# The first products of a hybrid encoder layer: backward gate first, forward gate in pieces of 256 and 272 columns, meta tokens normed ahead of the rows

## The chip, the core and the metric

The kernel runs on one core of a Trainium2 chip. The metric is the device time of one execution in microseconds (us), the median of several runs; shorter is better. Before the change the median of three runs is 1535.19 us (1533.58 to 1536.26). A profile is one further execution, recorded by the hardware.

Five engines work side by side, each through its own instructions in order: PE (TensorE, matrix products; its weight loads are listed apart as PEld), DVE (VectorE), ACT (ScalarE), POOL (GpSimd) and SP (SyncE, which here only starts transfers). PE writes to PSUM, eight banks of 128 partitions x 512 fp32 numbers; everything else lies in SBUF.

## What is computed

One layer: 16 learned meta tokens ahead of 1024 rows of width 1024, an RMSNorm, one wide input projection, neighbourhood attention beside a bidirectional gated recurrence (HGRN2), and an MLP. The change touches the first microseconds alone: the norm, and the two gate projections of the recurrence's first head.

```python
h = jnp.concatenate([meta_tokens, x], axis=1)          # 16 + 1024 rows
a = rms_norm(h, norm_mix)                              # h * rsqrt(mean(h*h) + eps) * g
(q_na, k_na, v_na, q_hg, z_f, z_b, i_hg, g_hg, gate_na, gate_hg) = split_cols(a @ w_in)

def gates(z, lb):                                      # z_f: 16 + 1024 rows, z_b: the 1024 rows
    log_f = logaddexp(log(lb), log1p(-lb) + log_sigmoid(z))
    return -expm1(log_f), log_f                        # k, and the log of the forget factor f
```

In the kernel f is `oml * sigmoid(z) + lb` and k is `oml * sigmoid(-z)`. The backward direction needs no meta rows, the forward direction does.

## The kernel before

The 1024 rows are kept as two halves of 512 tokens, normed and transposed: `aT[0]` and `aT[1]`, each a pair (high part in fp32r, and the rest, "low") of tiles 128 x 8 x 512; the first half has 64 more columns, of which 16 hold the meta tokens, behind the 512. A product of 128 output columns with n tokens is a sum over k = 0..7, and each k takes three matmuls into one PSUM bank: high weights x high tokens, high x low, low x high (`mm3`, L120 to L124). A block of 128 columns of `w_in` (512 KB) is loaded as `raw`; ACT copies it to `hi`, DVE or POOL makes `lo` of the difference.

`start` (L512) does what must come first. Rows arrive as eight tiles `xt[0..7]` of 128 rows, started by SP (L526), with the two gate blocks (forward `C_ZF`, then backward `C_ZB`) between the fourth and the fifth; the meta tokens are `xt[8]`, called `xm`, started by ACT (L528). For a tile, `square` sums its squares (ACT, L544, or DVE, L546), `root` takes the power -1/2 on POOL (L555), `scale` multiplies on DVE (L551), `turn` transposes on PE (L565), `evict` writes the high part from PSUM on ACT (L575) and the low part on DVE (L576). PE fills the time before the first rows are there with transposes of the identity into a bank nobody reads (`keep_warm`, L561): 36, and 6 ahead of each further tile.

Then, in the order in which the code is written (inside `manual_schedule` that order holds on every engine):

1. forward gate, first half: 8 k of 512 columns, with the transposes of chunks 6 and 7 of the first half between them (a chunk is one k of the four tiles of a half);
2. backward gate, first half: 6 k;
3. chunk by chunk the second half is transposed and evicted (chunk 0 to 7), with the last 2 k of the backward gate and the first 5 k of the forward gate's second half between the chunks; after the first chunk ACT evicts the first gate (two sigmoids, L220 and L221, from PSUM; DVE does the rest, L222 and L225), and after the fourth it squares the meta tokens;
4. the meta tokens are transposed (L656) and written to `aT[0]` (L657 to L659);
5. `rest` (L663): the remaining k of the forward gate's second half; the forward gate of the 16 meta tokens alone, 24 matmuls of 16 columns; the backward gate's second half, 8 k.

Behind that the first head's query projection (`C_Q`) and the rest of the kernel follow. Chunks of the second half go through the four banks of tag "a", so the transposes of chunk 4 wait until chunk 0's bank has been evicted by ACT and DVE, chunk 6 for chunk 2's, and so on. Two banks each have the tags "mm" and "mx".

Of the kernel before, what the change touches and what calls it, by code (L numbers as in the profile page):

```python
# [9 lines left out]
F32 = mybir.dt.float32  # L10
# [38 lines left out]
def layer(ctx: ExitStack, tc: tile.TileContext, x, meta, w_in, w_na, w_hg, w_o, w_up, w_dn,  # L49
# [23 lines left out]
    def bank(tag, name):  # L73
        return banks[tag].tile([P, 4, P], F32, tag=tag, name=name)
# [25 lines left out]
    def load_raw(src, kc):  # L100
        raw = wp.tile([P, KC, P], F32, tag="raw", name="raw")
        sp.dma_start(raw[:, :kc], src.rearrange("(k p) c -> p k c", p=P))
        return raw
# [17 lines left out]
    def mm3(ps, lh, ll, rh, rl, first, last):  # L121
        pe.matmul(ps, lh, rh, start=first, stop=False)  # L122
        pe.matmul(ps, lh, rl, start=False, stop=False)  # L123
        pe.matmul(ps, ll, rh, start=False, stop=last)  # L124
# [79 lines left out]
    def gates_of(hd, hp, tiles, done=()):  # L204
# [30 lines left out]
        if hd == 0:  # L235
            yield
            for n_ in range(5):
                d, ps, t0, n, nm = done[n_]
                ev, mev = gate(d)
                if nm:  # L240
                    mev(ps[:, n:])
                if n:
                    ev(ps[:, :n], t0, n)
                yield
            return
        zf = proj_steps(C_ZF + hd * P, *gate(0))
# [251 lines left out]

    firsts, blocks = [], {}

    def first_products(d, h, tag, n=TH):

        nm = NM if n == NM else 0
        c0 = TH if nm else 0
        ps = bank(tag, "mm").rearrange("p a b -> p (a b)")[:, :n]
        firsts.append((d, ps, h * TH, n - nm, nm))
        hi, lo = blocks[d]
        for k in range(KC):
            mm3(ps, hi[:, k], lo[:, k], *(q[:, k, c0:c0 + n] for q in aT[h]), k == 0, k == KC - 1)
            yield  # L510

    def start(gates):  # L512
# [12 lines left out]
        def load_x(i):  # L525
            sp.dma_start(xt[i][:, :D], x[i * P:(i + 1) * P, :])  # L526
# [2 lines left out]
        act.dma_start(g_col, g_mix)  # L529
        act.dma_start(lt.rearrange("p a b c -> p (a b c)"), lbl)  # L530
        act.dma_start(gain_sb, gain)
        for i in range(4):
            load_x(i)
        raws = [load_raw(w_in[:, c:c + P], KC) for c in (C_ZF, C_ZB)]
        for i in range(4, 8):
            load_x(i)

        def square(i, eng=act):
            t = xt[i]
# [38 lines left out]
        def some(steps, n):  # L578
            for _ in range(n):
                next(steps)  # L580

        def block(d):
            blocks[d] = [wp.tile([P, KC, P], F32R, tag=t, name=t) for t in ("hi", "lo")]
            act.copy(blocks[d][0], raws[d])

        def low(d, eng, c):
            hi, lo = blocks[d]
            eng.tensor_tensor(lo[:, c], raws[d][:, c], hi[:, c].bitcast(F32), op=ALU.subtract)
# [1 line left out]
        A, B = slice(0, 4), slice(4, 8)  # L590
        lts = lt.rearrange("p a b c -> p (a b c)")
        mh, ml = (t[:, :, TH:TH + NM] for t in aT[0])
        for k in range(6):
            pts[0, k] = bank("a" if k < 4 else "mx", "pt")
        for i in range(4):
            keep_warm(6 if i else 36)
            square(i)
            root(i)
            scale(i)
            turn(i, range(6))  # L600
        block(0)
        low(0, dve, A)
        f0 = first_products(0, 0, "mm")
        evict(0, 0)
        evict(0, 1)
        for k in range(6):
            some(f0, 1)
            if k < 2:
                chunk(0, k + 6)
            if k == 0:  # L610
                low(0, dve, B)
            evict(0, k + 2)
            if k == 0:
                block(1)
                low(1, pool, A)
                low(1, pool, B)
            if k == 3:
                dve.tensor_tensor(mx, lt[:, :, 0], lt[:, :, 1], op=ALU.max)
                for q in range(2):
                    pool.tensor_tensor(lt[:, :, q], lt[:, :, q], mx, op=ALU.subtract)  # L620
        some(f0, 2)
        square(4)
        root(4)
        act.activation(lts, lts, AF.Exp)
# [10 lines left out]
            scale(i)  # L635
        pool.tensor_tensor(lb_sb, lt[:, :, 0], mx, op=ALU.mult)
        pool.tensor_tensor(oml_sb, lt[:, :, 1], mx, op=ALU.mult)
        b0 = first_products(1, 0, "mx")
        some(b0, 6)
        f1 = first_products(0, 1, "mx")  # L640
        for k in range(KC):
            chunk(1, k)
            evict(1, k)
            if k == 0:
                next(gates)
            if k == 3:
                square(8)
                root(8)
                scale(8)
            if k < 2:  # L650
                some(b0, 1)
            if k > 2:
                some(f1, 1)
        ptm = bank("mm", "ptm")[:, 0].rearrange("p (k t) -> p k t", t=NM)
        for k in range(KC):
            pe.transpose(ptm[:, k], xt[8][:, k * P:(k + 1) * P], ident[:NM, :NM])  # L656
        dve.tensor_tensor(am, ptm, fap(g_col, 0, [[1, KC], [0, NM]]), op=ALU.mult)  # L657
        act.copy(mh, am)
        dve.tensor_tensor(ml, am, mh.bitcast(F32), op=ALU.subtract)  # L659
        p0s.close()  # L660
        return f1

    def rest(gates, f1):  # L663

        list(f1)
        next(gates)
        next(gates)
        list(first_products(0, 0, "mm", NM))
        next(gates)
        early[C_Q] = block_of(C_Q)  # L670
        list(first_products(1, 1, "mm"))
        next(gates)

    early = {}
# [971 lines left out]
```

## Time and profile before

| what | us |
|---|---|
| median of 3 runs | 1535.19 |
| the profiled execution, from outside | 1532.35 |
| its span in the trace | 1530.6 |
| PE busy | 1507.1 |
| DVE busy | 1029.2 |
| ACT busy | 657.9 |
| POOL busy | 379.6 |

The profiled execution took 1.75 us more than its span (1532.35 less 1530.6); times inside the trace count from the span's start. It was 2.84 us shorter than the median of the three timed runs, so a saving is worked out against its own time and then set against that median.

In rows of the timeline the columns are start in us, duration in us, engine, line, operation, output<-inputs, shape, count and, in brackets, the idle time just before with what ended it. The duration of a matmul has its pipeline in it: what one costs is read from start to start. Rows of one tile, or of one line, give the durations of a group as min/median/max in ns. A DMA row ends with the us from issue to landing. "SPq", "ACTq" are the issues of a transfer on SP and ACT.

### The profile page before, as it was taken

The page shows a single profiled execution, that of the slowest core. Times are in us where ns is not written, and L with a number is a line of the kernel's source. Part 1 is how long each engine was busy: PE and PEld are TensorE (multiplying, and loading weights), DVE is VectorE, ACT ScalarE, POOL GpSimd, SP SyncE. Part 2 cuts the span into 40 slices and gives each one's busy share as a digit, 9 for nine tenths or more (in the row PEclk, how much of TensorE's full clock was granted, in tenths as well). Part 3 has the DMA queues.
Part 4 walks back from the last instruction along what each step waited for, and adds up shares of the span by engine and source line. Part 5 has one row for each costly group of instructions (what it writes and reads, how often), then busy time and mean ns, then how long its engine had stood idle before and what let it go on. Part 6 is the DMA issues. An engine that isn't in the chain of part 4 may idle for free.

```text
span 1530.6 us, 23534 instructions
## 1 busy us (share of the span) xinstructions
PE 1507.1 (98%) x9242; PEld 1258.1 (82%) x9242; DVE 1029.2 (67%) x1602; ACT 657.9 (43%) x1168; POOL 379.6 (25%) x355
## 2 busy tenths in 40 slices
PE   9999999999999999999999999999999999999998
PEld 8888888878888887888888887888888888888886
DVE  6776666654876877666476358877777544877876
ACT  6231313125665676334133135455555533434444
POOL 3313131315414400011000122433344200231142
PEclk9999999999999999999999999999999999999999
DMA  4211111113123227445756123544444577573324
GB/s 167 59 29 43 42 44 32 54 35 124 61 69 113 80 69 251 137 131 164 256 163 222 46 92 117 175 153 153 152 154 154 209 261 235 192 233 111 96 83 151
DMA packets 142591, 195.61 MB, mean 128 GB/s; under 512 B 8192, under 2 KB 90240, under 8 KB 142480
## 3 DMA queue, kind: packets, MB, share of 16 engines
q1 hardware_dynamic: 133216, 172.53, 34.4%
q10 hardware_dynamic: 7088, 14.24, 2.4%
q0 software_dynamic: 2176, 7.34, 1.3%
q8 instruction: 72, 1.18, 0.3%
q14 instruction: 39, 0.32, 0.1%
HBM read 139.56 MB, written 54.53 MB: 127 GB/s over the span
## 4 chain that ended last, share of the span: by engine, by line
PE 90%; DVE 5%; issue 2%; ACT 2%; DMA 1%; POOL 1%; ACTq 0%; POOLq 0%; DVEq 0%
PE mm L122 11%; PE mm L123 11%; PE mm L124 11%; PE mm L1368 5%; PE pa L1368 4%; PE pb L875 4%; PE pb L876 4%; PE pb L877 4%; PE pb L1368 4%; PE pc L1368 4%; PE pc L876 3%; PE pc L875 3%; PE pc L877 3%; PE pa L877 2%; PE pa L876 2%
## 5 line engine op out<-in xcount | busy, mean ns | idle before, releaser
L122 PE MATMUL mm<-aT,hi 128*128 128x512 f32 (+2 forms) x640 | 230.2, 360 | 2.3 <-DVE QX L746 1.5
L124 PE MATMUL mm<-aT,lo 128*128 128x512 f32 (+2 forms) x640 | 226.8, 354 | 0.0
L123 PE MATMUL mm<-aT,hi 128*128 128x512 f32 (+2 forms) x640 | 226.0, 353 | 0.6 <-DVE aT L576 0.6
L122 PEld LDWEIGHTS mm<-aT,hi 128*128 128x128 f32 x640 | 120.7, 189 | 16.9 <-issue 1.7
L123 PEld LDWEIGHTS mm<-aT,hi 128*128 128x128 f32 x640 | 120.9, 189 | 13.7 <-DVE aT L576 1.2
L124 PEld LDWEIGHTS mm<-aT,lo 128*128 128x128 f32 x640 | 120.8, 189 | 13.4
L97 DVE TENSOR_TENSOR dl<-ur,dh 128x1024 fp32r<-128x1024 f32 x54 | 71.0, 1316 | 87.3 <-ACT dh L96 87.1
L96 ACT CAST dh<-ur 128x1024 fp32r<-128x1024 f32 x54 | 56.9, 1054 | 166.5 <-issue 91.1
L112 ACT CAST hi<-raw 128x1024 fp32r<-128x1024 f32 x34 | 35.7, 1051 | 96.7 <-PE mm L123 68.4
L1173 DVE TENSOR_TENSOR wl<-raw,wh 128x512 fp32r<-128x512 f32 x50 | 41.0, 824 | 36.4 <-ACT wh L1172 36.3
L1177 ACT ACTIVATE uv<-uv 128x512 f32<-128x512 f32 x48 | 30.4, 632 | 80.0 <-DVE uv L1285 48.9
L1173 DVE TENSOR_TENSOR wl<-sx,wh 128x512 fp32r<-128x512 f32 x70 | 61.1, 883 | 3.4 <-ACT wh L1172 3.3
L1172 ACT CAST wh<-sx 128x512 fp32r<-128x512 f32 x70 | 42.2, 619 | 42.4 <-PE pc L876 23.9
L1458 POOL TENSOR_TENSOR w<-w,tt 128x512 f32<-128x512 f32 x16 | 23.4, 1461 | 132.9 <-DVE tt L1457 113.2
L301 POOL TENSOR_TENSOR Y<-X,TN 128x512 f32<-128x512 f32 x20 | 34.2, 1711 | 84.6 <-DVE X L298 84.6
L801 DVE CUSTOM_DVE_ANT_0 pr<-nsc,NB 128x432 f32<-128x432 f32 (+1 forms) x64 | 35.1, 558 | 27.1 <-PE nsc L796 26.9
L113 DVE TENSOR_TENSOR lo<-raw,hi 128x1024 fp32r<-128x1024 f32 x34 | 45.3, 1334 | 9.1 <-ACT hi L112 8.9
L875 PE MATMUL pb<-nt,wh 128*128 128x512 f32 x128 | 50.2, 392 | 0.4 <-DVE uv L1255 0.2
L410 DVE TENSOR_TENSOR QQ<-QQ,TN 128x512 f32<-128x512 f32 x48 | 35.1, 741 | 22.9 <-PE sc L405 22.9
L122 PE MATMUL mm<-wh,mT 128*128 128x512 f32 x128 | 50.2, 392 | 0.0
L876 PE MATMUL pb<-nt,wh 128*128 128x512 f32 x128 | 49.8, 389 | 0.0
L124 PE MATMUL mm<-wh,mT 128*128 128x512 f32 x128 | 49.8, 389 | 0.0
(401 smaller groups left out, 4381.3 us busy)
## 6 DMA issues: line engine op xcount, KB each, us to landing
raw<-in_w_in SPq DMA_DIRECT2D x56, 512.0 KB, 4.0
ur<-usp SPq DMA_DIRECT2D x54, 512.0 KB, 3.5
raw<-in_w_up SPq DMA_DIRECT2D x16, 1024.0 KB, 6.0
usp<-us SPq DMA_DIRECT2D x60, 256.0 KB, 2.4
sg<-gsp SPq DMA_DIRECT2D x16, 512.0 KB, 3.8
w<-in_w_dn SPq DMA_DIRECT2D x16, 512.0 KB, 4.7
usp<-uv SPq DMA_DIRECT2D x30, 256.0 KB, 2.9
gsp<-gv ACTq DMA_DIRECT2D x24, 256.0 KB, 2.9
```

The lines of the kernel that those rows point to most:

```text
L96: act.copy(hi, src)
L97: dve.tensor_tensor(lo, src, hi.bitcast(F32), op=ALU.subtract)
L113: dve.tensor_tensor(lo[:, :kc], raw[:, :kc], hi[:, :kc].bitcast(F32), op=ALU.subtract)
L122: pe.matmul(ps, lh, rh, start=first, stop=False)
L123: pe.matmul(ps, lh, rl, start=False, stop=False)
L124: pe.matmul(ps, ll, rh, start=False, stop=last)
L875: pe.matmul(ps, lhs[0][:, c], rhs[0][:, k], start=first and k == 0, stop=False, skip_group_check=True)
L876: pe.matmul(ps, lhs[0][:, c], rhs[1][:, k], start=False, stop=False, skip_group_check=True)
L877: pe.matmul(ps, lhs[1][:, c], rhs[0][:, k], start=False, stop=k == 3, skip_group_check=True)
L1172: act.copy(v(hi), src)
L1173: dve.tensor_tensor(v(lo), src, v(hi).bitcast(F32), op=ALU.subtract)
L1368: pe.matmul(ps, a[n == 2][:, q, j * P:(j + 1) * P], b[n == 1][:, q], start=first and n == 0, stop=last and n == 2, skip_group_check=True)
```

## The change

- The first gate product is the backward gate's, of the first half (512 columns, 8 k). Its block is loaded first and split first, its low part on DVE; the forward gate's low part is made by POOL.
- The forward gate's first half is made in two pieces: the first 256 tokens, and the other 256 together with the 16 meta tokens (272 columns, a contiguous stretch of `aT[0]`). The piece of 16 columns is gone.
- For that the meta tokens must be in `aT[0]` early: they are squared (by DVE), scaled, transposed and split ahead of and between the four tiles of the first half. PE's identity transposes become 24, then the meta tokens' transposes, then 6 ahead of every tile.
- ACT starts with a square of 128 x 16 numbers of the identity, whose result nobody reads.
- In a k the three matmuls are ordered high x high, low weights x high tokens, high x low.
- The second half's chunks are transposed and evicted in pairs, with the forward gate's second piece (3 k, then 2 k) and twice 2 k of its second half between the pairs.
- Gates are evicted in the order in which they are made: five pieces with four sigmoid pairs of 512, 256, 256 and so on; the forward gate's first half now takes two pairs of 256.

```diff
-    def first_products(d, h, tag, n=TH):
+    def first_products(d, h, c0, n, nm=0, tag="mm"):
-        nm = NM if n == NM else 0
-        c0 = TH if nm else 0
-        ps = bank(tag, "mm").rearrange("p a b -> p (a b)")[:, :n]
-        firsts.append((d, ps, h * TH, n - nm, nm))
+        ps = bank(tag, "mm").rearrange("p a b -> p (a b)")[:, :n + nm]
+        firsts.append((d, ps, h * TH + c0, n, nm))
         for k in range(KC):
-            mm3(ps, hi[:, k], lo[:, k], *(q[:, k, c0:c0 + n] for q in aT[h]), k == 0, k == KC - 1)
+            rh, rl = (q[:, k, c0:c0 + n + nm] for q in aT[h])
+            pe.matmul(ps, hi[:, k], rh, start=k == 0, stop=False)
+            pe.matmul(ps, lo[:, k], rh, start=False, stop=False)
+            pe.matmul(ps, hi[:, k], rl, start=False, stop=k == KC - 1)
             yield
...
         act.dma_start(gain_sb, gain)
+        act.activation(am[:, 0], ident[:, :NM], AF.Square)
         for i in range(4):
             load_x(i)
-        raws = [load_raw(w_in[:, c:c + P], KC) for c in (C_ZF, C_ZB)]
+        raws = [wp.tile([P, KC, P], F32, tag="raw", name="raw") for _ in range(2)]
+        for d in (1, 0):
+            sp.dma_start(raws[d], w_in[:, (C_ZF, C_ZB)[d]:(C_ZF, C_ZB)[d] + P].rearrange("(k p) c -> p k c", p=P))
...
+        square(8, dve)
+        root(8)
+        scale(8)
+        keep_warm(24)
+        ptm = bank("mm", "ptm")[:, 0].rearrange("p (k t) -> p k t", t=NM)
+        for k in range(KC):
+            pe.transpose(ptm[:, k], xt[8][:, k * P:(k + 1) * P], ident[:NM, :NM])
         for i in range(4):
-            keep_warm(6 if i else 36)
+            keep_warm(6)
             square(i)
             root(i)
             scale(i)
             turn(i, range(6))
-        block(0)
-        low(0, dve, A)
-        f0 = first_products(0, 0, "mm")
+            if i == 0:
+                dve.tensor_tensor(am, ptm, fap(g_col, 0, [[1, KC], [0, NM]]), op=ALU.mult)
+            if i == 1:
+                dve.tensor_copy(mh, am)
+            if i == 2:
+                dve.tensor_tensor(ml, am, mh.bitcast(F32), op=ALU.subtract)
+        act.copy(blocks[1][0], raws[1])
+        low(1, dve, A)
+        b0 = first_products(1, 0, 0, TH)
...
-        b0 = first_products(1, 0, "mx")
-        some(b0, 6)
-        f1 = first_products(0, 1, "mx")
-        for k in range(KC):
-            chunk(1, k)
-            evict(1, k)
+        list(first_products(0, 0, 0, 256, 0, "mx"))
+        f0 = first_products(0, 0, 256, 256, NM, "mx")
+        some(f0, 3)
+        f1 = first_products(0, 1, 0, TH)
+        for k in range(0, KC, 2):
+            for q in (k, k + 1):
+                chunk(1, q)
+                evict(1, q)
             if k == 0:
                 next(gates)
-            if k == 3:
-                square(8)
-                root(8)
-                scale(8)
-            if k < 2:
-                some(b0, 1)
-            if k > 2:
-                some(f1, 1)
-        ptm = bank("mm", "ptm")[:, 0].rearrange("p (k t) -> p k t", t=NM)
-        for k in range(KC):
-            pe.transpose(ptm[:, k], xt[8][:, k * P:(k + 1) * P], ident[:NM, :NM])
-        dve.tensor_tensor(am, ptm, fap(g_col, 0, [[1, KC], [0, NM]]), op=ALU.mult)
-        act.copy(mh, am)
-        dve.tensor_tensor(ml, am, mh.bitcast(F32), op=ALU.subtract)
+            if k < 4:
+                some(f0, 3 - k // 2)
+            else:
+                some(f1, 2)
         p0s.close()
         return f1
     def rest(gates, f1):
         list(f1)
-        next(gates)
-        next(gates)
-        list(first_products(0, 0, "mm", NM))
-        next(gates)
+        for _ in range(3):
+            next(gates)
         early[C_Q] = block_of(C_Q)
-        list(first_products(1, 1, "mm"))
+        list(first_products(1, 1, 0, TH))
         next(gates)
```

Three places of the engines' orders follow. `warm` is the identity transpose, `ptm` the transposed meta tokens, `pt` a transposed chunk, `mm` a product's bank, `aT_87` and `aT_88` the high and low part of the first half, `aT_89` and `aT_90` those of the second.

PE at the very start, before:

```order
L561 MATMUL warm<-ident 128x128 x36
L565 MATMUL pt<-ident,xt 128x128 x6
L561 MATMUL warm<-ident 128x128 x6
L565 MATMUL pt<-ident,xt 128x128 x6
L561 MATMUL warm<-ident 128x128 x6
```

and now:

```order
L566 MATMUL warm<-ident 128x128 x24
L600 MATMUL ptm<-ident,xm 128x16 x8
L566 MATMUL warm<-ident 128x128 x6
L570 MATMUL pt<-ident,xt 128x128 x6
L566 MATMUL warm<-ident 128x128 x6
```

The meta tokens' eight transposes have moved from behind the second half's chunks to a place ahead of the first tile, with six identity transposes less around them; they wait for DVE's scaling of `xm`.

PE where the forward gate's meta columns are made: before, the last k of its second half and the first k of the 16 columns:

```order
L122 MATMUL mm<-aT_89,hi 128x512
L123 MATMUL mm<-aT_90,hi 128x512
L124 MATMUL mm<-aT_89,lo 128x512
L122 MATMUL mm<-aT_87,hi 128x16
L123 MATMUL mm<-aT_88,hi 128x16
L124 MATMUL mm<-aT_87,lo 128x16
```

and now, the last k of the forward gate's first piece and the first k of the second, both ahead of the second half's chunks:

```order
L507 MATMUL mm<-aT_87,hi 128x256
L508 MATMUL mm<-aT_87,lo 128x256
L509 MATMUL mm<-aT_88,hi 128x256
L507 MATMUL mm<-aT_87,hi 128x272
L508 MATMUL mm<-aT_87,lo 128x272
L509 MATMUL mm<-aT_88,hi 128x272
```

The 16 columns ride in 24 matmuls of 272 columns, and within a k the product with the low tokens, which DVE delivers last, comes third.

ACT in the second half's evictions (L575 and L580 write the high parts), before:

```order
L575 ACTIVATE aT_89<-pt,g_col 128x512
L220 ACT_TABLE_LOAD
L220 ACTIVATE sf<-mm 128x512
L221 ACTIVATE sn<-mm 128x512
L575 ACTIVATE aT_89<-pt,g_col 128x512 x3
L544 ACTIVATE junk,ssq<-xm 16x1025
L575 ACTIVATE aT_89<-pt,g_col 128x512 x4
L658 CAST aT_87<-am 128x8x16
```

and now:

```order
L580 ACTIVATE aT_89<-pt,g_col 128x512 x2
L220 ACT_TABLE_LOAD
L220 ACTIVATE sf<-mm 128x512
L221 ACTIVATE sn<-mm 128x512
L580 ACTIVATE aT_89<-pt,g_col 128x512 x6
L220 ACTIVATE sf<-mm 128x256
L221 ACTIVATE sn<-mm 128x256
L229 ACTIVATE fm<-mm 128x16
```

One more chunk is evicted ahead of the table load and the first sigmoids, and the meta tokens' square and copy are gone from ACT's queue here.

DVE's first instructions are now the square and the scaling of `xm`, ahead of the tiles'; between the four scalings stand the three small steps that write the meta tokens into `aT[0]`. POOL takes the power for `xm` first; the first half's key sum (`kd`, L287) comes on POOL behind all of the first gates. SP's transfers stand in the order they had, with the two gate blocks exchanged. Behind the first gates the rows of all five engines are the same as before, in the same order.

More of the change, by code (lines that the diff above doesn't have):

```diff
@@ L241, in gates_of @@
                     mev(ps[:, n:])
-                if n:
-                    ev(ps[:, :n], t0, n)
+                ev(ps[:, :n], t0, n)
                 yield
@@ L531, in start @@
         act.dma_start(gain_sb, gain)
+        act.activation(am[:, 0], ident[:, :NM], AF.Square)
         for i in range(4):
             load_x(i)
-        raws = [load_raw(w_in[:, c:c + P], KC) for c in (C_ZF, C_ZB)]
+        raws = [wp.tile([P, KC, P], F32, tag="raw", name="raw") for _ in range(2)]
+        for d in (1, 0):
+            sp.dma_start(raws[d], w_in[:, (C_ZF, C_ZB)[d]:(C_ZF, C_ZB)[d] + P].rearrange("(k p) c -> p k c", p=P))
         for i in range(4, 8):
             load_x(i)
+        for d in range(2):
+            blocks[d] = [wp.tile([P, KC, P], F32R, tag=t, name=t) for t in ("hi", "lo")]
         def square(i, eng=act):
@@ L580, in some @@
                 next(steps)
-        def block(d):
-            blocks[d] = [wp.tile([P, KC, P], F32R, tag=t, name=t) for t in ("hi", "lo")]
-            act.copy(blocks[d][0], raws[d])
         def low(d, eng, c):
@@ L606, in start @@
         for k in range(6):
-            some(f0, 1)
+            some(b0, 1)
             if k < 2:
@@ L610, in start @@
             if k == 0:
-                low(0, dve, B)
+                low(1, dve, B)
             evict(0, k + 2)
             if k == 0:
-                block(1)
-                low(1, pool, A)
-                low(1, pool, B)
+                act.copy(blocks[0][0], raws[0])
+                low(0, pool, A)
+                low(0, pool, B)
             if k == 3:
@@ L620, in start @@
                     pool.tensor_tensor(lt[:, :, q], lt[:, :, q], mx, op=ALU.subtract)
-        some(f0, 2)
+        some(b0, 2)
         square(4)
```

## Prediction

> **What bounds the kernel.** First the page: the span, the engines' busy times, and the chain of work that ended last.
>
> ```profile
> span 1530.6 us, 23534 instructions
> ...
> PE 1507.1 (98%) x9242; PEld 1258.1 (82%) x9242; DVE 1029.2 (67%) x1602; ACT 657.9 (43%) x1168; POOL 379.6 (25%) x355
> ...
> PE 90%; DVE 5%; issue 2%; ACT 2%; DMA 1%; POOL 1%; ACTq 0%; POOLq 0%; DVEq 0%
> ```
>
> PE is busy all but 23.5 us of the span and makes up 90% of the chain. So a microsecond of PE work or PE waiting that goes from the first stage shortens the kernel by one, if the others keep up right behind it. The view by stretches answers that (columns: stretch, its length, busy us and count of PE, PEld, DVE, ACT, POOL, granted clock, DMA share, GB/s):
>
> ```profile
> 40.00:45.00 5.00, 5.00 (x24) 4.09 (x23) 1.65 (x3) 0.96 (x2) 2.33 (x7) 1.00 0.30 83
> 45.00:62.00 17.00, 17.00 (x98) 14.96 (x96) 14.68 (x20) 4.16 (x6) 6.77 (x3) 1.00 0.15 43
> ```
>
> From 40 to 62 us PE never idles, so all that is removed before 40 us counts in full there; DVE is the next engine, with 2.3 us left of 17. Now the timeline of the stage that the change rewrites, from the first transposes of the second half on (PE, and ACT and DVE where PE waits for them):
>
> ```profile
> 23.20 1.58 DVE L551 TENSOR_SCALAR xt<-xt,rs 128x1024 f32<-128x1024 f32 x2
> ...
> 25.00 0.60 PE L565 MATMUL pt<-ident,xt 128*128 128x128 f32 x4
> ...
> 26.14 0.60 PE L565 MATMUL pt<-ident,xt 128*128 128x128 f32 x4
> ...
> 26.35 1.28 ACT L220 ACT_TABLE_LOAD   x1
> ...
> 28.61 1.85 ACT L575 ACTIVATE aT<-pt,g_col 128x512 fp32r<-128x512 f32 x3
> ...
> 29.35 2.07 DVE L576 SCALAR_TENSOR_TENSOR aT<-pt,g_col,aT 128x512 fp32r<-128x512 f32 x3
> ...
> 29.37 0.50 PE L122 MATMUL mm<-aT,hi 128*128 128x512 f32 x1
> ...
> 30.15 0.50 PE L123 MATMUL mm<-aT,hi 128*128 128x512 f32 x1 [0.28 <-DVE aT L576]
> ...
> 34.22 0.66 PE L656 MATMUL ptm<-ident,xm 16*128 16x16 f32 x8
> ...
> 34.81 0.50 PE L122 MATMUL mm<-aT,hi 128*128 128x512 f32 x1
> ...
> 36.99 0.17 PE L122 MATMUL mm<-aT,hi 128*128 128x16 f32 x1
> ...
> 39.58 0.49 PE L122 MATMUL mm<-aT,hi 128*128 128x512 f32 x1
> ...
> 45.17 0.39 PE L122 MATMUL mm<-aT,hi 128*128 128x512 f32 x1
> ...
> 56.05 0.28 PE L122 MATMUL mm<-aT,hi 128*128 128x256 f32 x1
> ...
> 62.02 0.76 PE L385 MATMUL sc<-q,kd 128*32 128x32 f32 x64
> ```
>
> Three things cost PE here: a wait at 29.37 to 30.15, because ACT loads a table and evicts a gate between two evictions; the meta tokens' transposes, 0.59 us from 34.22 to 34.81; and 24 matmuls of only 16 columns, 2.59 us from 36.99 to 39.58, or 0.108 each. From 45.17 to 56.05 stand 48 matmuls of 512 columns: 0.227 each, 5.44 for a product of 24. From 56.05 to 62.02 stand 24 of 256 and 24 of 272, at most 5.97 us: 0.124 each. So a matmul of 16 columns costs nearly what one of 256 does.
>
> **Term 1, from the second half's first chunk (T, 25.00 before) to the backward gate's second half (39.58).** Before: 14.58 us. A chunk with its change of operands costs 0.46 (25.00 to 26.14, less three matmuls of 0.227). After the change PE has 8 chunks (3.68), 15 matmuls of 272 (1.86) and 24 of 512 (5.44): 10.98 us. Ahead of T, 18 matmuls of 512 (4.08) become 24 of 256 and 9 of 272 (33 x 0.124 = 4.09): nothing. The gain is 14.58 - 10.98 = **3.6 us**, if nothing new waits; 2.06 of it is the pieces (5.44 + 2.59 against 5.97), the rest the transposes and the wait.
>
> What is late next? ACT evicts one more chunk (1.85 / 3 = 0.62) ahead of its table load, so the load starts at T + 1.97 where it was T + 1.35; evictions resume 2.26 later (26.35 to 28.61), DVE's 3.00 later at T + 4.97, then 0.69 each. PE is at chunk 6 at T + 5.99, which needs the bank of chunk 2, free at T + 5.66; at chunk 7 at T + 6.45, bank free at T + 6.35. It fits by 0.1 us. The last products come 0.68 apart and stay over 1 us behind DVE. If it didn't fit, the price is bounded by what the present wait costs, 0.28 (the row) to 0.55 (0.78 less one matmul); I take none. The forward gate in two halves gives ACT and DVE a second set of small instructions, and ACT, DVE and POOL take up the last gates and the `C_Q` block while PE runs 5.44 us of backward gate; there DVE is busy 1.65 of 5 us, ACT 0.96, so the gate work that moves there, an estimated 2 us (about what DVE does there now), is hidden. The key sum that moves behind the gates lies on POOL where it is busy 6.77 of 17 us. Without that cover DVE's 2 us would show.
>
> **Term 2, the first products.** Here is the front: the timeline; landings, in us from issue, of the two outer transfers on ACT's queue and of the fourth tile's rows; then that tile's issue, warm-up transposes and the DVE square.
>
> ```profile
> 0.73 0.42 ACTq L528 DMA_DIRECT2D xm<-in_meta  x1
> ...
> 1.65 7.01 PE L561 MATMUL warm<-ident 128*128 128x128 f32 x36 [1.65 <-POOL ident masks.py:199]
> ...
> 2.13 0.61 ACTq L531 DMA_DIRECT2D gain_sb<-in_gain  x1
> ...
> 4.88 1.28 ACT L544 ACT_TABLE_LOAD   x1 [4.88 <-DMA xt<-in_x]
> 6.17 1.06 ACT L544 ACTIVATE junk<-xt 128x1025 f32<-128x1025 f32 x1
> ...
> 7.40 0.56 POOL L555 TENSOR_TENSOR rs<-ssq,half 128x1 f32<-128x1 f32 x1 [5.81 <-ACT junk L544]
> 8.00 0.75 DVE L551 TENSOR_SCALAR xt<-xt,rs 128x1024 f32<-128x1024 f32 x1 [8.00 <-POOL rs L555]
> ...
> 8.44 0.72 POOL L555 TENSOR_TENSOR rs<-ssq,half 128x1 f32<-128x1 f32 x1 [0.47 <-ACT junk L544]
> ...
> 8.81 0.88 PE L565 MATMUL pt<-ident,xt 128*128 128x128 f32 x6 [0.15 <-DVE xt L551]
> ...
> 12.80 0.82 PE L565 MATMUL pt<-ident,xt 128*128 128x128 f32 x6
> ...
> 13.85 0.50 PE L122 MATMUL mm<-aT,hi 128*128 128x512 f32 x1 [0.23 <-ACT aT L575]
> ...
> 14.63 0.50 PE L123 MATMUL mm<-aT,hi 128*128 128x512 f32 x1 [0.29 <-DVE aT L576]
> ...
> 15.21 0.60 PE L565 MATMUL pt<-ident,xt 128*128 128x128 f32 x4
> ```
>
> ```profile
> xm<-in_meta ACTq DMA_DIRECT2D x1, 64.0 KB, 3.3
> gain_sb<-in_gain ACTq DMA_DIRECT2D x1, 2.0 KB, 6.9
> ```
>
> ```profile
> xt<-in_x SPq DMA_DIRECT2D x1, 512.0 KB, 6.7
> ```
>
> ```profile
> L526 SPq DMA_DIRECT2D xt<-in_x x1: 591/591/591, 2.1 to 2.1; - x1
> ...
> L561 PE MATMUL warm<-ident x3: 421/421/421, 6.6 to 7.0; 128*128 128x128 f32 x3
> L561 PE MATMUL warm<-ident x5: 272/272/273, 7.7 to 8.2; 128*128 128x128 f32 x5
> L546 DVE CUSTOM_DVE_ANT_0 junk<-xt x1: 1216/1216/1216, 19.9 to 19.9; 128x1025 f32<-128x1025 f32 x1
> ```
>
> At 13.85 the first product starts and at 14.63 its second matmul, held by DVE's low part. With that matmul third, one of 0.23 fills the wait: **0.24 us** (0 if the low weights are late too, at most 0.35).
>
> **Term 3, the start.** ACT's table load moves to 2.74 (the end of its last issue) and is over at 4.02; the small square costs nothing on the path, since the old load began only when the first rows had landed, at 4.88: it is hidden by that transfer. The first square is then 1.3 us earlier, but the fourth tile lands only at 2.1 + 6.7 = 8.8, so the squares follow the landings: the fourth is scaled at about 8.85 + 1.23 (6.17 to 7.40) + 0.56 to 0.97 + 0.75, or 11.7 at the latest. PE needs it later, because four turns take it 3.99 us from the first (8.81 to 12.80, 36 transposes of 0.111). So PE's own order sets the start. The meta chain: landing 4.03, square 1.22, power 0.56, scaling 0.75, with handovers about 6.75. Warm-up runs at two paces, seen in the durations 421 and 272: (7.01 - 8 x 0.11) / 28 = 0.219 slow, 0.11 fast from 7.6 us on. So 24 end at 1.65 + 24 x 0.219 = 6.9, the meta transposes (0.59 fast, 1.2 at half pace; I take 0.8) at 7.7, six fast ones at 8.36: the first turn at 8.4 where it was 8.81, **0.4 us** sooner. ACT's and DVE's chains to T shift with it: the last tile of the second half, scaled by 24.78 before, at 24.38; its transpose is wanted at 25.22 - 0.64 = 24.58.
>
> Here POOL's power of 8.44 ended at 9.16, 0.41 after DVE's scaling (8.00 to 8.75), while the first took 0.56 undisturbed. [...]
>
> **Sum**: 3.6 + 0.24 + 0.4 = 4.2 us. The profiled execution would take 1532.35 - 4.2 = 1528.1; against the median 1535.19, which is 2.84 above it, **1531.0**.
>
> **Rivals.**
> - *Half pace for longer.* For: the switch at 7.6 comes just when PE turns to the small meta transposes. Each transpose at the slow pace costs 0.108 more; if it stays slow through two more turns (18 transposes with their fill), 1.9 us go, the saving is 2.3 and the time 1532.9. Against: PE has no gap in the forecast. [...] The trace shows one switch alone, and the granted clock reads 1.00 throughout. Chance 0.17.
> - *The wait comes back at another bank.* The fit of 0.1 us at chunk 7 fails, and DVE's extra small gate pieces push the low parts: 0.55 there and up to 1 later, saving 2.6, time 1532.6. For: DVE is full behind 45 us. Against: its idle 3.3 us before. Chance 0.13.
> - *Slower: the meta chain holds everything.* Its landing now stands ahead of all of DVE's scalings and, through the meta transposes, of all of PE. Each us of delay costs one; it turns the sign from 4.2 us. If `xm` took the 6.9 us of the last transfer of the same queue, it would land 3.6 later, and PE, having idled, would repeat the slow pace for 18 transposes: 5.5 lost, 1.3 slower, 1536.5. Against: 3.3 in the row, first in its queue. Chance 0.04.
> - [...] Chance 0.06.
>
> **How the numbers follow.** The forecast has 0.60 (1530.2 to 1531.9). A measurement here tells about 0.2%, 3.07 us, from no change. Nine tenths of the forecast, a third of the first two rivals and all of the last pass it: 0.54 + 0.10 + 0.06 = 0.70 faster. The slower rival passes it only with 2 us more than its price, half its chance: 0.02 slower, and 0.28 within. The range reaches up over the first two rivals and down past the last, with the spread of the runs (1.3 either way): 1529.2 to 1533.6.
>
> **What would show it.** In the new profile: the table load before 4.1 us; the first turn at 8.4 and the first product at 13.45; T at 24.4; no matmul of 16 columns; the backward gate's second half at 35.3; PE dense from there. A first turn after 9.5, or an idle PE between T + 4.5 and T + 7, proves the first or second rival; a PE gap ahead of `ptm` the third. Shifts lost later, behind 45 us, would make the prediction wrong in a way that I hold for excluded.

## The result and the profile after

| | changed kernel | before |
|---|---|---|
| median of 15 runs each | 1530.59 us (1527.52 to 1533.88) | 1534.34 us (1532.03 to 1537.45) |
| profiled execution | 1530.97 us | 1532.35 us |
| its span | 1529.2 us | 1530.6 us |

The ratio is 0.9974, with a 95% interval of 0.9966 to 0.9982: 4.0 us less, between 2.8 and 5.2. The forecast was 4.2 less and 1531.0 us.

The page of the changed kernel, the lines on the span and the engines:

```profile
span 1529.2 us, 23532 instructions
...
PE 1503.1 (98%) x9236; PEld 1255.8 (82%) x9236; DVE 1034.4 (68%) x1608; ACT 657.4 (43%) x1168; POOL 377.6 (25%) x355
```

PE's busy time fell by 4.0 us (1507.1 to 1503.1), yet the span by only 1.4: in this pair of executions PE waits 2.6 us more somewhere. The view by stretches, with the columns of the prediction, says where it does not. Before:

```profile
14.00:25.00 11.00, 10.71 (x50) 8.58 (x51) 10.19 (x17) 8.16 (x15) 7.19 (x11) 1.00 0.53 174
25.00:40.00 15.00, 14.72 (x97) 12.33 (x96) 10.76 (x21) 10.81 (x21) 1.83 (x2) 1.00 0.01 2
```

and after:

```profile
14.00:25.00 11.00, 11.00 (x73) 9.98 (x74) 9.44 (x16) 7.83 (x15) 7.19 (x11) 1.00 0.52 172
25.00:40.00 15.00, 15.00 (x86) 13.03 (x86) 11.48 (x23) 10.03 (x20) 2.85 (x8) 1.00 0.01 2
40.00:57.00 17.00, 17.00 (x99) 15.05 (x97) 14.50 (x20) 4.17 (x6) 6.76 (x3) 1.00 0.24 67
```

From 14 us to 57 us PE no longer idles; the two waits of before, 0.29 and 0.28, are not in these stretches any more. The second is gone. The first now lies ahead of 14 us and is partly filled: from the first product's start to the matmul that needs the low tokens were 0.78 us with one matmul of 0.23 in them (13.85 to 14.63), and are 0.79 with two (13.10 to 13.89 in the timeline below). The timeline of the changed kernel, at the places that the prediction named:

```profile
2.85 1.28 ACT L532 ACT_TABLE_LOAD   x1 [2.85 <-issue]
4.13 1.22 DVE L551 CUSTOM_DVE_ANT_0 junk<-xm 16x1025 f32<-16x1025 f32 x1 [4.13 <-DMA xm<-in_meta]
5.43 1.37 POOL L560 TENSOR_TENSOR rs<-ssq,half 16x1 f32<-16x1 f32 x2 [3.84 <-DVE ssq L551]
...
6.02 0.74 DVE L556 TENSOR_SCALAR xm<-xm,rs 16x1024 f32<-16x1024 f32 x1 [0.67 <-POOL rs L560]
...
6.82 0.66 PE L600 MATMUL ptm<-ident,xm 16*128 16x16 f32 x8 [0.49 <-DVE xm L556]
6.84 0.75 DVE L556 TENSOR_SCALAR xt<-xt,rs 128x1024 f32<-128x1024 f32 x1
...
7.41 0.88 PE L566 MATMUL warm<-ident 128*128 128x128 f32 x6
...
8.12 0.82 PE L570 MATMUL pt<-ident,xt 128*128 128x128 f32 x6
...
13.10 0.50 PE L507 MATMUL mm<-aT,hi 128*128 128x512 f32 x1 [0.23 <-ACT aT L580]
13.44 0.40 PE L508 MATMUL mm<-aT,lo 128*128 128x512 f32 x1
13.89 0.51 PE L509 MATMUL mm<-aT,hi 128*128 128x512 f32 x1
...
14.23 0.60 PE L570 MATMUL pt<-ident,xt 128*128 128x128 f32 x4
...
23.96 1.03 PE L570 MATMUL pt<-ident,xt 128*128 128x128 f32 x8
...
25.88 1.28 ACT L220 ACT_TABLE_LOAD   x1
...
28.14 3.64 ACT L580 ACTIVATE aT<-pt,g_col 128x512 fp32r<-128x512 f32 x6
...
28.87 4.04 DVE L581 SCALAR_TENSOR_TENSOR aT<-pt,g_col,aT 128x512 fp32r<-128x512 f32 x6
...
29.88 1.10 PE L570 MATMUL pt<-ident,xt 128*128 128x128 f32 x8
...
34.92 0.39 PE L507 MATMUL mm<-aT,hi 128*128 128x512 f32 x1
...
40.36 0.39 PE L122 MATMUL mm<-aT,hi 128*128 128x512 f32 x1
...
57.21 0.76 PE L384 MATMUL sc<-q,kd 128*32 128x32 f32 x64
```

The first score matmul (`sc`), the end of what the change touches, comes at 57.21 where it came at 62.02: 4.81 us are gained in front. In three parts: first product 13.85 to 13.10, 0.75; from there to the second half's first chunk (T) 11.15 to 10.86, 0.29; from T to `sc` 37.02 to 33.25, 3.77.

So 3.4 us are lost behind `sc` in this pair. Two marks behind it enclose the loss: the first score matmul of the attention (`nsc`), and the first product of the MLP (`pa`). The timeline of the changed kernel has, at these two:

```profile
367.46 0.29 PE L799 MATMUL nsc<-KS,QX 128*128 128x288 f32 x1
...
899.51 0.39 PE L879 MATMUL pa<-nT,wh 128*128 128x512 f32 x1
```

At `nsc` the kernel is 4.8 us ahead of before (367.46 against 372.23 in before's timeline), at `pa` 1.3 (899.51 against 900.85), and behind it the distance stays. Between the marks the two kernels have the same instructions in the same order on every engine. Is that the change's doing, or do executions differ there? That was the first question.

### The profile page after: what moved, and what is told of

It reads as the page before. It is cut to its first block, busy times and chain, and to the rows that moved or that the text cites. A ratio compares the mean times of both kernels' runs of the same rounds, so it can differ in the third digit from the quotient of the medians.

```text
span 1529.2 us, 23532 instructions
## 1 busy us (share of the span) xinstructions
PE 1503.1 (98%) x9236; PEld 1255.8 (82%) x9236; DVE 1034.4 (68%) x1608; ACT 657.4 (43%) x1168; POOL 377.6 (25%) x355
## 4 chain that ended last, share of the span: by engine, by line
PE 89%; DVE 5%; issue 2%; ACT 2%; DMA 1%; POOL 0%; POOLq 0%; ACTq 0%; SPq 0%; DVEq 0%
PE mm L122 11%; PE mm L123 10%; PE mm L124 10%; PE mm L1372 5%; PE pa L1372 4%; PE pb L879 4%; PE pb L880 4%; PE pb L881 4%; PE pb L1372 4%; PE pc L1372 4%; PE pc L879 3%; PE pc L881 3%; PE pc L880 3%; PE pa L879 2%; PE pa L880 2%
## 5 line engine op out<-in xcount | busy, mean ns | idle before, releaser
L122 PE MATMUL mm<-aT,hi 128*128 128x512 f32 (+2 forms) x600 | 214.7, 358 | 2.8 <-DVE QX L750 1.5
L124 PE MATMUL mm<-aT,lo 128*128 128x512 f32 (+2 forms) x600 | 212.2, 354 | 0.0
L123 PE MATMUL mm<-aT,hi 128*128 128x512 f32 (+2 forms) x600 | 211.2, 352 | 0.0
L122 PEld LDWEIGHTS mm<-aT,hi 128*128 128x128 f32 x600 | 113.2, 189 | 16.1 <-issue 1.7
L124 PEld LDWEIGHTS mm<-aT,lo 128*128 128x128 f32 x600 | 113.2, 189 | 12.5
L123 PEld LDWEIGHTS mm<-aT,hi 128*128 128x128 f32 x600 | 113.3, 189 | 11.7
```

## The experiments

Each kernel below has one profiled execution. Times from the trace are compared by place, since the stretch between the two marks makes the whole span too coarse. The marks of all profiles (us; "product" is the first product, "nsc to pa" the stretch just named):

| profile | switch to the full pace | first turn | product | T | `sc` | T to `sc` | nsc to pa |
|---|---|---|---|---|---|---|---|
| before | 7.55 | 8.81 | 13.85 | 25.00 | 62.02 | 37.02 | 528.6 |
| before, again | 7.54 | 8.65 | 13.69 | 24.84 | 61.87 | 37.03 | 531.2 |
| before + early table | 7.74 | 8.59 | 13.57 | 24.72 | 61.76 | 37.03 | 528.5 |
| changed | 5.45 | 8.12 | 13.10 | 23.96 | 57.21 | 33.25 | 532.0 |
| changed, again | 6.36 | 8.21 | 13.19 | 24.02 | 57.31 | 33.30 | 533.3 |
| old order of the three matmuls | 6.78 | 8.21 | 13.19 | 24.26 | 57.54 | 33.28 | 529.2 |
| no early table | 6.21 | 8.68 | 13.72 | 24.57 | 57.85 | 33.28 | 528.4 |
| 3 fill transposes | 5.01 | 7.90 | 13.29 | 24.11 | 57.41 | 33.30 | 528.4 |
| gate after chunk 0 | 5.26 | 8.16 | 13.35 | 24.17 | 58.46 | 34.29 | 530.5 |
| forward gate first | 4.94 | 8.17 | 13.27 | 26.26 | 59.45 | 33.19 | 529.8 |
| piece of 16 | 7.11 | 8.32 | 13.30 | 24.07 | 61.70 | 37.63 | 528.0 |
| piece of 16, again | 7.71 | 8.57 | 13.55 | 24.33 | 61.97 | 37.65 | 529.9 |
| piece of 128 | 6.47 | 8.15 | 13.13 | 23.90 | 59.93 | 36.03 | 528.3 |

The first column is from the trace's record of PE's granted clock, which begins with this switch; the first identity transpose at the full pace follows within 0.11 us where no other transposes stand between (7.62 in the first row).

### Each kernel once more: the stretch in the middle

No edit.

> The kernel before, unchanged, profiled once more. The first profiles of before and after differ by 4.81 us at the start of the query projection (45.17 and 40.36 us) but only by 1.4 us in span; 3.4 us were given back between 400 and 860 us, where both kernels issue the same instructions. Theory A (the middle varies from one execution to the next, whatever the kernel): this profile agrees with the first one of before within 0.6 us at the query projection (the pace of the warm-up transposes may differ), but its own middle, 400 to 860 us, differs from the first one's by 1 us or more. Theory B (the earlier front puts the middle into a worse phase, so the loss belongs to the change): this middle agrees with the first one's within 0.3 us.

> The changed kernel, profiled a second time. Theory A (what follows the first head differs from execution to execution of one program by 2 to 3 us, as the two profiles of the kernel before showed): the first score matmul comes again at 57.2, within 0.3, the first product at 13.1 to 13.3, and the end is anywhere from 1520 to 1524 (1521.7 in the first profile). Rival (the changed kernel itself gives back 3 us between 380 and 460 us): the operations at 460 us and behind come within 0.5 us of the first profile's, so the end is 1521.2 to 1522.2.

The timeline of the kernel before, in its second profile:

```profile
372.36 0.29 PE L795 MATMUL nsc<-KS,QX 128*128 128x288 f32 x1
...
903.51 0.39 PE L875 MATMUL pa<-nT,wh 128*128 128x512 f32 x1
```

The same program took 531.2 us between the marks where it had taken 528.6, and its span was 1533.2 us (1530.6 the first time). The changed kernel took 532.0 and 533.3, and its span was 1531.0 the second time. Over all profiles the stretch took 528.0 to 533.3. The ten with the changed front have a mean of 529.8, the three with the old one 529.4. So the middle differs by up to 2.6 us between executions of one program, and the front of the two kernels doesn't decide it; the small gain of the first pair of profiles was such a draw. What differs is above all how long PE waits: its gaps between the marks sum to 5.4 and 7.4 us in the two profiles of before, to 8.2 and 9.1 in those of the changed kernel, and to 4.7 to 9.1 over all thirteen. Nearly all of it is waiting for DVE or ACT, and why the waits differ is not shown. The front repeats much better: `sc` at 62.02 and 61.87, then at 57.21 and 57.31, 4.6 to 4.8 apart. That both profiles of the unedited changed kernel lie high in the middle stays open: the interval of the timed ratio (2.8 to 5.2) leaves room for a loss of up to 1.9 us there, and for none. For the same reason a single span doesn't rank the kernels below: four of them with a later front (old order, no early table, 3 fill transposes, piece of 128) have spans of 1526.2 to 1528.2 us, less than both of the changed kernel, but the 15 timed runs of the changed kernel alone have spans from 1525.8 to 1532.1.

### The piece of 16 columns, back

```diff
-            for n_ in range(5):
+            for n_ in range(6):
...
-                ev(ps[:, :n], t0, n)
+                if n:
+                    ev(ps[:, :n], t0, n)
...
-        f0 = first_products(0, 0, 256, 256, NM, "mx")
+        f0 = first_products(0, 0, 256, 256, 0, "mx")
...
     def rest(gates, f1):
         list(f1)
         for _ in range(3):
             next(gates)
+        list(first_products(0, 0, TH, 0, NM))
+        next(gates)
```

> The changed kernel with the meta columns on their own again: 256, 256, and 24 matmuls of 16 columns behind the forward gate's second half; all else as changed. Theory (a matmul of 16 columns costs nearly what one of 256 does): 24 x 0.108 = 2.6 us more, less about 24 x 0.005 = 0.1 for 256 in place of 272, so the query projection starts 2.5 us later relative to the first turn than in the changed kernel. Rival (the small matmuls hide waits of DVE and ACT that the changed kernel has there anyway): 1 us or less.

T to `sc` grew by 4.4 us (33.25 to 37.63), not by 2.5. The timeline of the kernel with the piece shows two costs: 24 matmuls of 16 columns from 35.10 to 37.70, 2.60 us, and then this:

```profile
37.59 0.26 PE L510 MATMUL mm<-aT,hi 128*128 128x16 f32 x1
37.70 0.66 PE L508 MATMUL mm<-aT,hi 128*128 128x512 f32 x1
38.16 0.63 PE L509 MATMUL mm<-aT,lo 128*128 128x512 f32 x1
38.58 0.63 PE L510 MATMUL mm<-aT,hi 128*128 128x512 f32 x1
...
41.43 0.39 PE L508 MATMUL mm<-aT,hi 128*128 128x512 f32 x1
```

The nine matmuls of 512 columns from 37.70 to 41.43 stand 0.41 apart, not 0.227: 3.73 us for 2.04, 1.69 lost. In the view by stretches the granted clock, behind POOL's count, is 0.98 and then 0.59:

```profile
34.00:38.00 4.00, 4.00 (x31) 3.81 (x30) 1.61 (x6) 1.20 (x4) 1.30 (x1) 0.98 0.02 6
38.00:42.00 4.00, 4.00 (x12) 3.11 (x12) 1.66 (x3) 1.07 (x3) 2.32 (x7) 0.59 0.10 25
```

2.60 and 1.69 make 4.29 of the 4.38. The first is what Term 1 used for the piece (2.59); the second was in no theory. Two more kernels looked at it: the same once more, and one whose 24 matmuls have 128 columns instead of 16 (the edit against the kernel with the piece; nobody reads the 112 further columns).

```diff
-                if n:
+                if n > 112:
...
-        list(first_products(0, 0, TH, 0, NM))
+        list(first_products(0, 0, TH - 112, 112, NM))
```

> The kernel with the 16 meta columns as a piece of their own, once more. Theory (the stretch of 24 small matmuls slows what follows it): the nine or so matmuls of 512 columns behind the piece stand 0.43 apart again instead of 0.227, and the first score matmul comes 37.4 to 37.8 behind the second half's first chunk. Rival (the half pace behind it was a chance of that execution): all matmuls behind the piece stand 0.227 apart and the distance is 35.8 to 36.1, 2.6 to 2.8 more than the changed kernel's 33.25.

> As the kernel with the piece of 16 columns, but the 24 matmuls of that piece have 128 columns: 112 token columns more, computed a second time, which nobody reads. Theory (few columns a matmul slow what follows: the array works for a sixth of the time): with 128 columns each the 24 take 2.6 to 2.9 us, and the matmuls of 512 behind them stand 0.227 apart; the distance from the second half's first chunk to the first score matmul is 35.8 to 36.2. Rival (chance, or any stretch of short matmuls): half pace behind it as with 16 columns, 37.4 to 38.0.

With 16 columns the half pace came again: granted clock 0.57 from 38 to 42 us, and T to `sc` 37.65. With 128 columns it didn't. The timeline of that kernel:

```profile
34.91 0.22 PE L508 MATMUL mm<-aT,hi 128*128 128x128 f32 x1
...
37.54 0.45 PE L508 MATMUL mm<-aT,hi 128*128 128x512 f32 x1
...
37.83 0.39 PE L509 MATMUL mm<-aT,lo 128*128 128x512 f32 x1
```

The 24 take 2.63 us, no more than those of 16 columns, the clock is 1.00 behind them, and T to `sc` is 36.03: 2.78 more than without the piece, as its 2.63 nearly say. So a stretch of matmuls with few columns, back to back, can be followed by half pace (0.59 and 0.57 here) although the profile shows no gap on PE, and the number of columns seems to count: at 0.227 us for 512 columns, 16 columns are an estimated 7 ns of work in each 108 ns, 128 columns 57 in each 110. (By this estimate the array works a fifteenth of the time with 16 columns, not the sixth that the expectation has.) In the kernel before, the same 24 were followed by full pace in all three profiles with the old front. The last section shows what is different there: where the stretch lies among slots of 3.413 us, counted from the switch to the full pace.

### The order of the three matmuls, undone

```diff
-            pe.matmul(ps, lo[:, k], rh, start=False, stop=False)
-            pe.matmul(ps, hi[:, k], rl, start=False, stop=k == KC - 1)
+            pe.matmul(ps, hi[:, k], rl, start=False, stop=False)
+            pe.matmul(ps, lo[:, k], rh, start=False, stop=k == KC - 1)
```

> The changed kernel with the old order of the three matmuls in a k (high x high, high x low, low weights x high). Theory: the first product's second matmul waits for DVE again and one matmul of 0.23 no longer fills that wait, so the transposes behind the first k start 0.23 to 0.35 later relative to the first product (1.13 us in the changed kernel, 1.36 before), and the query projection 0.2 later. Rival (the transposes or the tile scaling bind there): no difference at the second half's first chunk.

The timeline of this kernel has the old wait again:

```profile
13.19 0.50 PE L507 MATMUL mm<-aT,hi 128*128 128x512 f32 x1 [0.23 <-ACT aT L580]
13.97 0.50 PE L508 MATMUL mm<-aT,hi 128*128 128x512 f32 x1 [0.28 <-DVE aT L581]
14.31 0.39 PE L509 MATMUL mm<-aT,lo 128*128 128x512 f32 x1
14.54 0.49 PE L570 MATMUL pt<-ident,xt 128*128 128x128 f32 x3
```

From the first product to the transposes behind it are 1.35 us, against 1.13 (13.10 to 14.23) with the new order, and `sc` is 0.2 to 0.3 later. The order is worth 0.22 us, one matmul of 512 columns.

### The table: alone on the kernel before, and taken out of the changed one

Alone:

```diff
         act.dma_start(gain_sb, gain)
+        act.activation(am[:, 0], ident[:, :NM], AF.Square)
```

> The kernel before with the small square of the identity at the head of ACT's queue and nothing else, so the activation table is loaded before the rows land. Theory (PE's 36 warm-up transposes and then 4 x 12 transposes set the front): the first tile is scaled 1.2 us sooner, but the first turn comes only when the 36 are done, at 8.5 to 8.8 if the slow pace lasts to 7.6 us, at 7.5 to 7.8 if it ends at 5.3 us as in the profile of the changed kernel; a gain of 0 to 0.3 or of about 1. Rival (ACT's square chain is what the front waits for, whatever PE's pace): the first turn and the first product come 1.2 us sooner in any case.

Taken out:

```diff
         act.dma_start(gain_sb, gain)
-        act.activation(am[:, 0], ident[:, :NM], AF.Square)
```

> The changed kernel without the small square of the identity, so the table is loaded when the first rows have landed, as before. Theory (with the short warm-up the front now waits for data, so the early load is worth what the first turn shows): the squares start at 6.2, 7.2, 8.3, 9.3 us as before, the first turn comes at 8.8 in place of 8.1 to 8.3, the first product at 13.7 to 13.8 in place of 13.1 to 13.3: 0.5 to 0.6 us later. Rival (PE's own order sets the front, as forecast): less than 0.2.

On the kernel before, the first tile was scaled at 6.60 instead of 8.00, but the first turn came at 8.59 (8.81 and 8.65 without): the 36 identity transposes ended just then, and the early data waited for PE. The first product gained 0.1 to 0.3. In the changed kernel without the square, the timeline reads otherwise:

```profile
4.75 1.28 ACT L548 ACT_TABLE_LOAD   x1 [4.75 <-DMA xt<-in_x]
...
7.87 0.75 DVE L555 TENSOR_SCALAR xt<-xt,rs 128x1024 f32<-128x1024 f32 x1 [1.16 <-POOL rs L559]
...
8.68 0.33 PE L569 MATMUL pt<-ident,xt 128*128 128x128 f32 x1 [0.45 <-DVE xt L555]
```

The table load again begins when the rows have landed, the first tile is scaled at 7.87 instead of 6.84, and now PE waits 0.45 us for it. First turn 8.68 (8.12 and 8.21 with the table), first product 13.72 (13.10 and 13.19), `sc` 57.85 (57.21 and 57.31): 0.5 to 0.6 lost against these two profiles. The other kernels with the early table and six fills have the first product at 13.13 to 13.55, so the loss could be as little as 0.2. The same square is worth 0.1 to 0.3 beside 36 identity transposes and 0.5 to 0.6 beside the shorter PE order, which makes the data the later of the two.

### Fewer fill transposes

```diff
-            keep_warm(6)
+            keep_warm(3)
```

> The changed kernel with 3 identity transposes ahead of each of the four tiles in place of 6. Theory (PE's padding holds the four turns 0.35 us behind the data: the fourth tile is scaled at 11.7, its turn came at 12.05): the fourth turn moves to 11.7 to 11.8, the first product to 12.75, and the query projection starts 0.3 earlier. Rival (the padding keeps the fast pace, or the first weight block binds): no gain, or matmuls at half pace behind the turns.

The first turn came earlier (7.89), the first product didn't (13.28). The timeline:

```profile
9.56 1.06 ACT L549 ACTIVATE junk<-xt 128x1025 f32<-128x1025 f32 x1 [0.75 <-DMA xt<-in_x]
...
12.18 0.33 PE L570 MATMUL pt<-ident,xt 128*128 128x128 f32 x1 [0.70 <-DVE xt L556]
```

The fourth tile's square waited for its rows until 9.56 (9.08 in the changed kernel's profile), and PE waited 0.70 for that tile. So the landing of the fourth tile's rows set the first product here: 9.47 us, and over all profiles they landed between 8.84 and 9.58, a spread of more than the 0.35 to be gained. Two kernels with all six fills had it as late (9.53 with the gate behind one chunk, 9.46 with the forward gate first), and their first product at 13.35 and 13.27. What less filling is worth when the rows land early is therefore not shown. None of these kernels beats the changed one in front.

### The first gate's eviction behind one chunk instead of two

```diff
             for q in (k, k + 1):
                 chunk(1, q)
                 evict(1, q)
-            if k == 0:
-                next(gates)
+                if q == 0:
+                    next(gates)
```

> The changed kernel with the first gate evicted between the second half's chunks 0 and 1, as before, in place of behind chunk 1. Theory (it is the place of the table load and of the sigmoids among the evictions that decides): chunk 1's low part comes at T + 5.0, the transposes of chunk 5, which need its bank, are wanted at T + 4.1, so PE waits 0.8 to 0.9 us there and the query projection starts 0.5 to 0.9 later relative to T than in the changed kernel. Rival (pairing the chunks took the wait away by itself): no difference.

```profile
25.52 1.28 ACT L220 ACT_TABLE_LOAD   x1
...
28.51 0.75 DVE L581 SCALAR_TENSOR_TENSOR aT<-pt,g_col,aT 128x512 fp32r<-128x512 f32 x1
...
29.31 0.33 PE L570 MATMUL pt<-ident,xt 128*128 128x128 f32 x1 [0.88 <-DVE aT L581]
```

With the table load at T + 1.35, as before the change, DVE resumes with one chunk less done, and the transposes of the third pair stand 0.88 us for a bank (the bracket in the last row). T to `sc` is 34.29, 1.0 more. So it is the one chunk more ahead of the table load that keeps PE dense, and the fit that the forecast gave 0.1 us did hold.

### The forward gate first

The two gates change places, with their loads and splits: the forward gate's 256 columns come first, beside the first half's evictions, and the backward gate's 512 second.

```diff
-        for d in (1, 0):
+        for d in (0, 1):
...
-        act.copy(blocks[1][0], raws[1])
-        low(1, dve, A)
-        b0 = first_products(1, 0, 0, TH)
+        act.copy(blocks[0][0], raws[0])
+        low(0, dve, A)
+        b0 = first_products(0, 0, 0, 256)
...
-        list(first_products(0, 0, 0, 256, 0, "mx"))
+        list(first_products(1, 0, 0, TH, 0, "mx"))
```

> The changed kernel with the forward gate's piece of 256 first and the backward gate's 512 second. Theory (the first product runs while chunks are evicted at 0.7 us each; 3 matmuls of 512 take 0.68, 3 of 256 only 0.36, so PE waits 0.3 per chunk): the first 8 k end at about 19.3 as evictions do, and the second half's first chunk comes at 25.8 in place of 24.0 to 24.2, with the query projection 1.5 to 1.8 later. Rival (the second half's first chunk is held by DVE's scaling, which ends at 24.0 anyway): no difference.

T came at 26.26, 2.2 to 2.3 later than in the changed kernel, and `sc` 2.1 to 2.2 later, more than the 1.5 to 1.8 expected. The timeline shows the pace of the first piece (L509 is the k's third matmul, which needs the low tokens from DVE):

```profile
15.98 0.39 PE L509 MATMUL mm<-aT,hi 128*128 128x256 f32 x1
...
16.74 0.39 PE L509 MATMUL mm<-aT,hi 128*128 128x256 f32 x1
...
17.40 0.39 PE L509 MATMUL mm<-aT,hi 128*128 128x256 f32 x1
```

They stand 0.66 to 0.76 apart, the pace of DVE's evictions (four of them took 2.82 us from 15.18); PE's own work for such a k is 0.37. With 512 columns a k is 0.68 of work, and the evictions hide behind it. That is what putting the backward gate's chain first is for: without it the pieces would have given back half of the gain.

## Why the prediction was right

**Term 1, 3.6 us forecast: right.** From T to the backward gate's second half the forecast had 10.98; the rows have 23.96 to 34.92, 10.96. ACT's table load came at T + 1.92 (T + 1.97 forecast), DVE's evictions resumed at T + 4.91 (T + 4.97), the fourth pair's transposes started at T + 5.92 (T + 5.99), and PE waited nowhere. Behind 40 us DVE is now busy 14.50 of 17 us with what moved there, and PE covers it all. T to `sc` gained 3.77, 0.17 over the term: the backward gate's second half took 40.36 - 34.92 = 5.44 us, where it had taken 5.59 behind the small matmuls. The experiment with the piece of 16 columns gave its price back at 2.60, and the gate behind one chunk gave the wait back.

**Term 2, 0.24 forecast: right,** 0.22 by undoing it. The rest of the 0.29 to 0.32 between the first product and T is in the two pieces ahead of T, which were put at nothing: their 33 matmuls took 4.01 us (19.95 to 23.96) where 18 of 512 columns had taken 4.08.

**Term 3, 0.4 forecast: right in sum, wrong in one step.** The first product came 0.75 earlier in the first pair of profiles and 0.50 in the second. The step that failed is that "PE's own order sets the start"; by it the early table has no term of its own in the sum, yet without the square 0.5 to 0.6 are lost. The forecast took the switch of PE's pace at 7.6, where it had been; it came at 5.5, PE was early and waited 0.49 for `xm`, and the first turn came at 8.12, right behind the meta transposes and six fast fills. With a late switch (7.71, piece of 16, again) the first turn is at 8.57, later than the 8.4 forecast. So the start is set by the meta chain when the switch is early, by PE's pace when it is late, and both lie within 0.5 us. The sum near 0.4 was therefore in part luck. The meta chain itself ran as forecast: `xm` scaled at 6.76 (6.75 forecast).

The first tile's power on POOL and DVE's scaling of `xm` both ran from 6.02. The power took 0.78 us, where the one for `xm` alone had taken 0.55, and ended at 6.80, 0.04 behind DVE's end (6.76). Why it takes longer beside the scaling is not shown. The first turn's data came at 7.59.

**The rivals.** *Half pace for longer* came in a small form in one profile, 0.45 at the first turn (8.57 against 8.12). *The wait at another bank* didn't come. *The meta chain* left its mark, the gap of 0.49 us ahead of `ptm`, but no price against the forecast's 8.4. It did set the first turn: in the second profile `xm` was scaled 0.09 later (6.85), and `ptm`, the first turn and the first product each came 0.09 later. The last chance, 0.06, was for more than the forecast's gain, and that is where the front ended, 4.6 to 4.8. The timed ratio doesn't tell it from the forecast's 4.2.

**What the forecast left out.** "PE dense from there" held to the end of the first head, and the step from there to the end of the kernel assumed that the same instructions take the same time. Between one execution and the next they don't, by 2 to 3 us, so that one profile of each side would have shown a gain of 1.4. The median over 15 runs does what the pair can't. That the timed 4.0 and the forecast 4.2 agree to 0.2 is still closer than the runs can bear out: the interval is 2.8 to 5.2, the front alone gained 4.6 to 4.8, and the forecast time of 1531.0 rests on a median of 1535.19, for which 15 runs gave 1534.34.

## What to carry to other kernels

Price a narrow matmul by what a wide one costs, and let its columns ride in a neighbour: 24 of 16 columns alone cost 2.60 us and were followed by half pace in two of the five profiles that have them, while 512 and 16 columns in pieces of 256 and 272 cost 0.53 more than the 512 alone (5.97 against 5.44). When an engine's table load or first small step can begin under a transfer, its worth depends on which of the two, data or engine order, comes last (0.1 to 0.3 us on the kernel before, 0.5 to 0.6 in the changed one): test it with the version that it is to go into, not with the one before. For a change in one stage, compare marks at the stage's two ends over two profiles, and leave the span to the timed runs.

## What the hardware showed besides

- **Half pace in the middle of a busy PE.** Behind 24 matmuls of 16 columns the granted clock fell to 0.59 and 0.57 over 4 us, in two profiles of two; behind 24 of 128 columns it stayed at 1.00. In each of the thirteen traces, every later switch to half pace stands a whole number of 3.413 us behind the first switch to the full pace (9 of them in the two with the piece of 16, 167 in the kernel before). So the time behind the first switch is read here in slots of 3.413 us. Two slots of the kernel with the piece of 16, around its 24 matmuls (35.10 to 37.70):

```profile
34.42:37.83 3.41, 3.41 (x29) 3.29 (x28) 1.19 (x4) 1.08 (x2) 1.30 (x1) 1.00 0.01 2
37.84:41.24 3.40, 3.40 (x10) 2.63 (x10) 1.66 (x3) 1.19 (x3) 2.32 (x7) 0.50 0.00 0
```

  The whole stretch of 2.60 us lies in one slot, here and in the second profile, and the next slot has half pace (0.50 above). In the three profiles with the old front the stretch lies across the end of a slot, with at most 1.74 us in one (in the kernel before 1.28 and 1.32), and no half pace follows. The piece of 128 has 2.28 of its 2.63 us in one slot and none follows either; as its place differs too, this one profile doesn't show by itself that the columns decide.
- **The same behind a wait.** In the kernel before PE waits 2.41 us for DVE until 577.70. Behind it the clock is 0.50 from 578 to 581 us, a further switch beside the one that the prediction saw. That happened in nine of the thirteen profiles, whichever the kernel, and is one part of what varies in the middle: from the place that the kernel before reaches at 572 us to the one that it reaches at 592, the four profiles without it take 1.6 us less than its first.

```profile
574.00:578.00 4.00, 1.59 (x12) 1.27 (x11) 3.08 (x5) 3.13 (x6) 0.00 (x0) 0.95 1.03 355
578.00:581.00 3.00, 3.00 (x12) 2.53 (x11) 2.67 (x5) 1.70 (x4) 0.00 (x0) 0.50 0.60 213
```

  The wait itself is in all thirteen, at 2.35 to 2.41 us. What differs is again its place: in the nine, PE idled 2.07 to 2.35 us in one slot; in the four others the wait lies across the end of one, and no slot has more than 1.66. In all thirteen traces, from the first switch to the end of the kernel, each slot with 2.07 us or more of gaps on PE was followed by half pace, and none with 1.76 or less was, other than those that the matmuls of 16 columns fill.
- **The start's pace.** PE's first transposes began at 1.65 us in all profiles, but the switch to the full pace came anywhere from 4.94 to 7.74. The view's granted clock reads 1.00 ahead of it too, because the clock's record begins with the switch: 1.00 from 1.7 to 7.0 us in the kernel before, at 0.213 from one transpose to the next, and 1.00 from 8 to 12, at 0.11. From the first transpose to the switch are 3.29 to 6.09 us, and what sets its place is not shown. Among the changed kernels that have the early table and all fill transposes the first product moved by 0.45 at most (13.10 to 13.55).
